# Two products instead of three in the channel-major gemms, full-height score and decay products, and a hand-written start, in a three-layer hybrid block

## The chip, the cores and the metric

One core of a Trainium2 chip runs the whole program; the other cores are idle. The metric is device time in microseconds (us) of one execution. A run of the kernel before was timed three times: 1604.77, 1605.06 and 1608.36 us, median 1605.06. A separate execution was profiled.

## The reference, cut to what matters

The model has 256 tokens of width 1024 and batch 1. Two layers each do `x + 0.5*swiglu(norm(x))`, a mixer, and a second half-weight swiglu; the hidden width is 2816. The first mixer is a gated linear recurrence with 4 heads, the second is attention in a window of 128 tokens with 16 query heads and 2 key heads of width 64; both also attend to 256 memory tokens. A third layer is a state-space scan with 32 heads in 4 groups, beside a short convolution, followed by one more swiglu. All of it is fp32. These lines are the ones that the change touches:

```python
# first mixer: scores with a running maximum of the gates
log_d = b[..., :, None] - b[..., None, :] + ic[..., None, :]
s = jnp.einsum('bhjd,bhsd->bhjs', qc, kc) * jnp.exp(log_d - m_t[..., None])
# second mixer, per block of 128 queries: 8 query heads share a key head
s = jnp.einsum('bqhgd,bkhd->bhgqk', qn, kn)
# third layer: causal convolutions, and decays within the scan
xbc = jax.nn.silu(causal_depthwise_conv(xbc, ssd_conv_w) + ssd_conv_b)
seg = acum[:, :, None] - acum[:, None, :]
decay = jnp.exp(jnp.where(causal, seg, -jnp.inf))
v = causal_depthwise_conv(s_c * s_x, sconv_w)
```

## The kernel before, in words

Every weight matrix is read once from HBM, in 520 or so chunks of up to 512 KB, by SP's queue into five `raw` buffers (`load`, lines 312 to 319). `prepare` (lines 321 to 330) splits a chunk: ACT rounds it to the fast format fp32r (`whi`), DVE subtracts to get the remainder (`wlo`); there are nine buffers of each. Activations are split the same way. A product of two split numbers is made of three products, hi by hi, hi by lo and lo by hi, added up in PSUM.

There are three kinds of gemm. `gemm` (line 392) is token-major: it loads 128x128 of the activations as the stationary operand and streams 512 columns of weights past it, three times (lines 423 to 425). `gemm_ch` (line 434) is channel-major: the weights are stationary, and 256 tokens are streamed. Its three products for one tile of 128 channels are lines 445 to 447, and it goes through the four chunks in order, k-tile by k-tile, with all four tiles of 128 channels open in two PSUM banks; the evacuation functions get these banks at the end of the call. It is called 14 times: for a_q and a_k of the first mixer (lines 915 and 916), and for B, C, xs0 to xs3 and two times three parts of `sconv` in the third layer. `gemm_hidden` (line 564), used by the gated feed-forward (`ffn_in`), is channel-major too, but goes tile by tile: for one tile it passes through all four chunks, with one product of 512 columns (weights' hi by the operand's hi and lo side by side, line 574) and one of 256 (weights' lo by the operand's hi, line 575). One bank then holds two halves, which `both_parts` adds: a copy on ACT (line 600) and an addition on DVE.

`bank(mm)` gives one of four PSUM banks for gemms, and four more serve all else (`sm`). 31 slots of 128x512 in SBUF serve activations.

Order of work: the program is written out as one list. Elementwise and small matrix work of the mixers stands in generators that `tick` and `pump` advance, so that it is interleaved with the gemms at a set pace (`pace`), and `defer` puts a step off by a number of ticks. The framework's scheduler then orders each engine's queue by these places and by when it expects operands to be ready; a later instruction with free operands can be put ahead. What is decided at build time stays: each engine works its queue in order.

Around the small products that the change touches: `score_head` (line 854) broadcasts a head's gate maxima with a product of four rows (line 857, fp32, which goes as two passes). `swa_units` (line 1039) makes scores by products of 64 rows, one per head (line 1061, fp32, two passes); even and odd heads lie on the lower and upper 64 partitions, and a unit takes heads of one parity; the keys lie twice in `bkt`, once for each half (line 1022). `ssd_unit` (line 1266) spreads the cumulated decays of two heads to all partitions with two products of 64 rows (line 1278): `act_t` holds a hi and a lo part of each of 32 heads, and `pick` selects and adds them.

The first instructions (lines 751 to 776): SP loads token block 0 of x, the gain row, the first chunks and block 1; TensorE does 8 warm-up products, the products that spread the gain row (line 766), and 12 more; `norm_residual` norms and splits both token blocks; `ffn_in` begins with a group of 8 chunks (`FIRST`), first for token block 0, then for block 1.

Of the kernel before, what the change touches and what calls it, by code (L numbers as in the profile page):

```python
# [10 lines left out]
F32 = mybir.dt.float32  # L11
# [6 lines left out]
P = 128  # L18
# [67 lines left out]
def hybrid_kernel(ctx: ExitStack, tc: tile.TileContext, *aps, names=None):  # L86
# [58 lines left out]
    act.copy(out=identr, in_=ident)  # L145
# [175 lines left out]
    def prepare(upto):  # L321
        while prepared[0] < min(upto, len(plan)):
            c = plan[prepared[0]]
            load(prepared[0] + RAW)
            prepared[0] += 1
            c.hi = wpool.tile([P, 1024], F32R, tag="whi", bufs=WBUFS, name=nm("whi"))
            c.lo = wpool.tile([P, 1024], F32R, tag="wlo", bufs=WBUFS, name=nm("wlo"))
            n = max(off + w for _, _, off, w in c.entries)
            act.copy(out=c.hi[:, 0:n], in_=c.raw[:, 0:n])  # L329
            tt(c.lo[:, 0:n], c.raw[:, 0:n], c.hi[:, 0:n].bitcast(F32), ALU.subtract)  # L330
# [102 lines left out]

    def gemm_ch(chunks, xop, evac):

        ps = [bank(mm), bank(mm)]
        nk = 8
        for c in chunks:
            need(c)
            for kt, key, off, n in c.entries:  # L440
                xh, xl = xop.mov(kt)
                for j in range(n // P):
                    o = ps[j // 2][:, (j % 2) * SEQ:(j % 2 + 1) * SEQ]
                    wh, wl = c.hi[:, off + j * P:off + (j + 1) * P], c.lo[:, off + j * P:off + (j + 1) * P]
                    pe.matmul(out=o, lhsT=wh, rhs=xh, start=kt == 0 and j % 2 == 0, stop=False)  # L445
                    pe.matmul(out=o, lhsT=wh, rhs=xl, start=False, stop=False)  # L446
                    pe.matmul(out=o, lhsT=wl, rhs=xh, start=False, stop=kt == nk - 1 and j % 2 == 1)  # L447
                tick()
            used[0] += 1
        for i in range(2):  # L450
            evac(i, ps[i])
# [112 lines left out]
    def gemm_hidden(chunks, xop, tiles, evac):  # L564


        for i in range(tiles):
            ps = bank(mm)
            for c in chunks:
                if i == 0:  # L570
                    need(c)
                for kt, _, off, _ in c.entries:
                    sl = slice(off + i * P, off + (i + 1) * P)
                    pe.matmul(out=ps, lhsT=c.hi[:, sl], rhs=xop.both(kt), start=kt == 0, stop=False)  # L574
                    pe.matmul(out=ps[:, 0:SEQ], lhsT=c.lo[:, sl], rhs=xop.mov(kt)[0], start=False, stop=kt == 7)  # L575
                if i == tiles - 1:
                    used[0] += 1
# [870 lines left out]
```

## Time and profile before

| | |
|---|---|
| runs | 1604.77, 1605.06, 1608.36 us; median 1605.06 |
| the profiled execution | 1604.94 us, span 1603.2 us |
| TensorE matmuls | 1583.9 us busy, 99% of the span, 8664 records |
| weight loads (PEld) | 1355.3 us, 85% |
| DVE, ACT, POOL | 65%, 55%, 2% of the span |
| HBM | 176 GB/s over the span |

The span goes from the first to the last instruction; the execution's own time also holds what lies outside it. PE is TensorE, PEld its weight loads, which run beside the products. Products are pipelined: each is recorded with its whole latency, so that neighbours overlap, and the cost of one in a dense stream is the distance to the next start. An fp32 product appears as two records. In a timeline equal neighbours are merged, with their number behind the x; a bracket tells how long the engine stood idle before the row and what ended it.

### The profile page before, as it was taken

To read this page: it belongs to the slowest core of one execution; us is meant where nothing else is said; L and a number is where in the kernel's file an instruction comes from. 1 tells how busy PE (TensorE), PEld (TensorE's weight loads), DVE (VectorE), ACT (ScalarE), POOL (GpSimd) and SP (SyncE) were. 2 spreads that over 40 slices of the span, in tenths; PEclk is the share of its full clock that TensorE was granted. 3 is DMA by queue.
4 is the path that set the end of the run, shared out by engine and by line. 5 is a ranking of instruction groups with operands and counts; after the bars stand their busy time and mean duration, and the time that the engine had idled before them with its cause. 6 is when DMAs were issued, how large, how long until landed. Compare 5 with 4: busy or idle time off the path is not lost.

```text
span 1603.2 us, 22953 instructions
## 1 busy us (share of the span) xinstructions
PE 1583.9 (99%) x8664; PEld 1355.3 (85%) x8664; DVE 1037.7 (65%) x1632; ACT 886.1 (55%) x1430; POOL 39.7 (2%) x72
## 2 busy tenths in 40 slices
PE   8999999999999999999999999999999999999998
PEld 7888897788888888887788888889899988888886
DVE  6676475657765567747765676468788864577662
ACT  6665365546655455635565655357855653456542
POOL 1000000100000000001100000000000000000000
PEclk9999999999999999999999999999999999999999
DMA  8656374446556546564323666465455566565560
GB/s 281 196 179 229 117 261 143 151 132 210 174 194 223 179 163 202 193 215 165 119 79 115 200 200 223 143 217 180 146 157 154 151 195 185 157 211 170 197 223 28
DMA packets 126467, 282.89 MB, mean 176 GB/s; under 512 B 11774, under 2 KB 23186, under 8 KB 126356
## 3 DMA queue, kind: packets, MB, share of 16 engines
q1 hardware_dynamic: 126356, 281.43, 54.6%
q8 instruction: 68, 1.11, 0.3%
q14 instruction: 43, 0.35, 0.1%
HBM read 280.34 MB, written 1.05 MB: 176 GB/s over the span
## 4 chain that ended last, share of the span: by engine, by line
PE 93%; DVE 2%; issue 1%; DMA 1%; ACT 1%; POOL 1%; SPq 0%; POOLq 0%; DVEq 0%; ACTq 0%
PE ps L574 20%; PE ps L423 15%; PE ps L425 15%; PE ps L424 15%; PE ps L575 11%; PE ps L445 3%; PE ps L446 3%; PE ps L447 3%; PE ps L458 2%; PE ps L1061 1%; PE ps L1303 1%; PE ps L676 1%; POOL t L517 1%; DVE wlo L122 1%; PE ps L1083 1%
## 5 line engine op out<-in xcount | busy, mean ns | idle before, releaser
L122 DVE TENSOR_TENSOR wlo<-raw,whi 128x1024 fp32r<-128x1024 f32 (+1 forms) x521 | 626.2, 1212 | 228.9 <-ACT whi L329 222.3
L329 ACT CAST whi<-raw 128x1024 fp32r<-128x1024 f32 (+1 forms) x521 | 537.5, 1042 | 321.8 <-PE ps L425 226.6
L574 PE MATMUL ps<-xt,whi 128*128 128x512 f32 x1440 | 500.6, 392 | 0.0
L575 PE MATMUL ps<-xt,wlo 128*128 128x256 f32 x1440 | 403.2, 280 | 0.0
L574 PEld LDWEIGHTS ps<-xt,whi 128*128 128x128 f32 x1440 | 269.4, 187 | 59.1
L423 PE MATMUL ps<-whi,s 128*128 128x512 f32 x696 | 277.4, 400 | 0.3 <-ACT s L1380 0.3
L424 PE MATMUL ps<-wlo,s 128*128 128x512 f32 x696 | 274.4, 394 | 0.0
L425 PE MATMUL ps<-whi,s 128*128 128x512 f32 x696 | 274.1, 394 | 0.0
L575 PEld LDWEIGHTS ps<-xt,wlo 128*128 128x128 f32 x1440 | 272.2, 189 | 0.2
L122 DVE TENSOR_TENSOR s<-ps,s 128x256 f32<-128x256 f32 (+1 forms) x218 | 101.3, 468 | 120.3 <-ACT s L600 100.8
L423 PE MATMUL ps<-whi,xt 128*128 128x512 f32 (+2 forms) x448 | 174.2, 389 | 3.2 <-ACT xt L460 1.8
L425 PE MATMUL ps<-whi,xt 128*128 128x512 f32 (+2 forms) x448 | 170.1, 381 | 1.2 <-DVE xt L122 1.2
L424 PE MATMUL ps<-wlo,xt 128*128 128x512 f32 (+2 forms) x448 | 169.8, 379 | 0.0
L423 PEld LDWEIGHTS ps<-whi,s 128*128 128x128 f32 x696 | 130.8, 188 | 31.4 <-DVE s L122 0.8
L425 PEld LDWEIGHTS ps<-whi,s 128*128 128x128 f32 x696 | 130.7, 188 | 30.7
L424 PEld LDWEIGHTS ps<-wlo,s 128*128 128x128 f32 x696 | 130.9, 188 | 28.7
L445 PE MATMUL ps<-xt,whi 128*128 128x256 f32 x448 | 129.1, 288 | 0.0
L122 DVE TENSOR_TENSOR s<-s,s 128x256 f32<-128x256 f32 (+2 forms) x228 | 107.7, 478 | 32.5 <-ACT s L616 18.0
L446 PE MATMUL ps<-xt,whi 128*128 128x256 f32 x448 | 127.0, 284 | 0.0
L447 PE MATMUL ps<-xt,wlo 128*128 128x256 f32 x448 | 126.8, 284 | 0.0
L600 ACT COPY s<-ps 128x256 f32<-128x256 f32 x180 | 66.2, 368 | 86.7 <-PE ps L575 84.8
L423 PEld LDWEIGHTS ps<-whi,xt 128*128 128x128 f32 x448 | 84.4, 188 | 19.9 <-ACT xt L460 2.2
(218 smaller groups left out, 1369.3 us busy)
## 6 DMA issues: line engine op xcount, KB each, us to landing
raw<-in_ffn_w_in_dram SPq DMA_DIRECT2D x160, 512.0 KB, 4.9
raw<-in_ffn_w_out_dram SPq DMA_DIRECT2D x88, 512.0 KB, 4.5
raw<-in_w_in_dram SPq DMA_DIRECT2D x80, 512.0 KB, 3.9
raw<-in_a_w_in_dram SPq DMA_DIRECT2D x24, 512.0 KB, 4.4
raw<-in_w_down_dram SPq DMA_DIRECT2D x22, 512.0 KB, 4.8
raw<-in_ffn_w_in_dram SPq DMA_DIRECT2D x32, 256.0 KB, 4.5
raw<-in_w_ssd_proj_dram SPq DMA_DIRECT2D x16, 512.0 KB, 3.6
raw<-in_w_gate_dram SPq DMA_DIRECT2D x16, 512.0 KB, 5.0
```

The source lines that it names most:

```text
L122: (eng or dve).tensor_tensor(out=o, in0=a, in1=b, op=op)
L329: act.copy(out=c.hi[:, 0:n], in_=c.raw[:, 0:n])
L423: pe.matmul(out=o, lhsT=xh, rhs=wh, start=first, stop=False)
L424: pe.matmul(out=o, lhsT=xh, rhs=wl, start=False, stop=False)
L425: pe.matmul(out=o, lhsT=xl, rhs=wh, start=False, stop=last)
L445: pe.matmul(out=o, lhsT=wh, rhs=xh, start=kt == 0 and j % 2 == 0, stop=False)
L446: pe.matmul(out=o, lhsT=wh, rhs=xl, start=False, stop=False)
L447: pe.matmul(out=o, lhsT=wl, rhs=xh, start=False, stop=kt == nk - 1 and j % 2 == 1)
L458: pe.transpose(out=ps[:, i * P:(i + 1) * P], in_=src[:, i * P:(i + 1) * P], identity=ident)
L574: pe.matmul(out=ps, lhsT=c.hi[:, sl], rhs=xop.both(kt), start=kt == 0, stop=False)
L575: pe.matmul(out=ps[:, 0:SEQ], lhsT=c.lo[:, sl], rhs=xop.mov(kt)[0], start=False, stop=kt == 7)
L600: act.copy(out=dst, in_=ps[:, SEQ:2 * SEQ])
```

## The change

`gemm_ch` becomes a wrapper around the tile-by-tile loop, now called `gemm_tiles`; each tile is evacuated by `parts_sum` into an SBUF slot, and the former evacuation functions read the slot. The products for decays, gate maxima and scores get 128 rows: with cleared rows in `m_t`, `acs`, `act_t`, `pick`, and with keys in cleared tiles `kpad`, where the keys of one head half stand in 64 rows of one column block and again in the other 64 rows of a second block, so that one product serves two heads. Scores now work with hi and lo parts (three fp32r products). `identr` is filled later. The first instructions of TensorE, ACT and DVE are kept in the order written; the gain row is loaded from ACT's queue; `x`'s second block is loaded ahead of chunks 2 to 4; the first `ffn_in` begins with a group of 3 chunks, then one chunk at a time.

```diff
     def prepare(upto):
         while prepared[0] < min(upto, len(plan)):
...
+            prepare_hi()()
+
+    def prepare_hi():
...
+        act.copy(out=c.hi[:, 0:n], in_=c.raw[:, 0:n])
+        return lambda: tt(c.lo[:, 0:n], c.raw[:, 0:n], c.hi[:, 0:n].bitcast(F32), ALU.subtract)
...
+    def parts_sum(dst, ps):
+
+        act.copy(out=dst, in_=ps[:, SEQ:2 * SEQ])
+        tt(dst, ps[:, 0:SEQ], dst, ALU.add)
+
+    def gemm_tiles(chunks, xop, tiles, evac):
+
+
+        for i in range(tiles):
+            ps = bank(mm)
+            for n_c, c in enumerate(chunks):
+                if i == 0:
+                    need(c)
+                for n_k, (kt, _, off, _) in enumerate(c.entries):
+                    sl = slice(off + i * P, off + (i + 1) * P)
+                    pe.matmul(out=ps, lhsT=c.hi[:, sl], rhs=xop.both(kt), start=kt == 0, stop=False)
+                    pe.matmul(out=ps[:, 0:SEQ], lhsT=c.lo[:, sl], rhs=xop.mov(kt)[0], start=False, stop=kt == 7)
+                if i == tiles - 1:
+                    used[0] += 1
+                if n_c == 1 or n_c == 3:
+                    tick()
+            evac(i, ps)
+
     def gemm_ch(chunks, xop, evac):
...
+        pair = []
+
+        def tile_evac(i, ps):
+            if i % 2 == 0:
+                pair.append(slot())
+            parts_sum(pair[-1][:, (i % 2) * SEQ:(i % 2 + 1) * SEQ], ps)
+            if i % 2 == 1:
+                evac(i // 2, pair[-1])
+        gemm_tiles(chunks, xop, 4, tile_evac)
...
-    def ffn_in(blocks, xop):
+    def ffn_in(blocks, xop, ahead=FIRST):
...
-        gemm(blocks[0], xop, evac, [blocks[0][0:FIRST], blocks[0][FIRST:]] if FIRST < 8 else [blocks[0]])
+        gemm(blocks[0], xop, evac, [blocks[0][0:ahead]] + [[c] for c in blocks[0][ahead:]])
...
-        nc.sync.dma_start(out=g_row[j * 32:j * 32 + 1, :], in_=A["ffn1_norm_g"][0:1, j * 512:(j + 1) * 512])
-    prepare(2)
+        nc.scalar.dma_start(out=g_row[j * 32:j * 32 + 1, :], in_=A["ffn1_norm_g"][0:1, j * 512:(j + 1) * 512])
+    load(2)
     load_x(1)
+    load(RAW)
...
+    with tc.manual_schedule(engines={mybir.EngineType.PE, mybir.EngineType.Activation, mybir.EngineType.DVE}):
+        warm_up(WARM[0])
...
+        warm_up(WARM[1])
+        halves = {}
+        normed(res_half(0), gains, halves.__setitem__)
+        for j in range(2):
+            low = prepare_hi()
+            split_t(halves[j], 4, [xop.hi[j][:, :, 0, :], xop.lo[j][:, :, 0, :]])
+            xop.filled.add((0, j))
+            low()
+        act.copy(out=identr, in_=ident)
+        norm_residual(1, gains, xop)
...
-    h = ffn_in(S["f1in0"], xop)
+    h = ffn_in(S["f1in0"], xop, 3)
...
-    def q_evac(i, ps):
-        s = slot()
-        act.activation(out=s, in_=ps, func=AF.Copy, scale=float(P) ** -0.5)
+    def q_evac(i, s):
+        act.activation(out=s, in_=s, func=AF.Copy, scale=float(P) ** -0.5)
...
-        pe.matmul(out=bc[:, 0:SEQ], lhsT=ident[0:4, hh:hh + 1].to_broadcast([4, P]), rhs=m_t[0:4, 0:SEQ],
+        pe.matmul(out=bc[:, 0:SEQ], lhsT=ident[:, hh:hh + 1].to_broadcast([P, P]), rhs=m_t[:, 0:SEQ],
...
+    kpad = [[slot(F32R).rearrange("p (u t) -> p u t", u=2) for _ in range(2)] for _ in range(2)]
+    for kp in kpad[0] + kpad[1]:
+        pool_e.memset(kp.bitcast(F32), 0.0)
...
+            for u in range(2):
+                rows_u = slice(64 * u, 64 * u + 64)
+                for g in range(2):
+                    kh, kl = (kp[rows_u, u, t * P:(t + 1) * P] for kp in kpad[g])
+                    kt = tk[rows_u, g * P:(g + 1) * P]
+                    act.copy(out=kh, in_=kt)
+                    tt(kl, kt, kh.bitcast(F32), ALU.subtract)
...
+                qh, ql = slot(F32R), slot(F32R)
+                act.copy(out=qh, in_=tq)
+                tt(ql, tq, qh.bitcast(F32), ALU.subtract)
...
-        sets = [[h0 + par + 2 * i for i in range(per)] for h0 in range(0, 8, 2 * per) for par in range(2)]
+        sets = [list(range(h0, h0 + per)) for h0 in range(0, 8, per)]
...
+            for i in range(0, per, 2):
+                pair = slice((hs[i] // 2) * P, (hs[i] // 2 + 1) * P)
+                o2 = s[:, i * w:(i + 2) * w].rearrange("p (a b) -> p a b", a=2)
+                pe.matmul(out=o2, lhsT=qh[:, pair], rhs=kh, start=True, stop=False)
+                pe.matmul(out=o2, lhsT=qh[:, pair], rhs=kl, start=False, stop=False)
+                pe.matmul(out=o2, lhsT=ql[:, pair], rhs=kh, start=False, stop=True)
...
-            pe.matmul(out=sb[:, i * SEQ:(i + 1) * SEQ], lhsT=pick[:, hd:hd + 1].to_broadcast([64, P]), rhs=act_t,
+            pe.matmul(out=sb[:, i * SEQ:(i + 1) * SEQ], lhsT=pick[:, hd:hd + 1].to_broadcast([P, P]), rhs=act_t,
...
-        def sc_evac(i, ps):
-            s = slot()
-            act.copy(out=s, in_=ps)
+        def sc_evac(i, s):
             pr.append(s)
```

## Rows read from the trace of the kernel before

**Rows 1.** The page: busy time of each engine, and the chain that ended last.

```profile
PE 1583.9 (99%) x8664; PEld 1355.3 (85%) x8664; DVE 1037.7 (65%) x1632; ACT 886.1 (55%) x1430; POOL 39.7 (2%) x72
PE 93%; DVE 2%; issue 1%; DMA 1%; ACT 1%; POOL 1%; SPq 0%; POOLq 0%; DVEq 0%; ACTq 0%
```

**Rows 2.** Windows: length, then PE, PEld, DVE, ACT, POOL busy; clock, DMA share, GB/s.

```profile
1180.00:1260.00 80.00, 79.96 (x631) 75.86 (x631) 70.63 (x125) 51.35 (x90) 4.96 (x5) 1.00 0.54 154
...
213.00:238.00 25.00, 22.68 (x187) 22.00 (x187) 20.90 (x48) 14.85 (x22) 1.57 (x2) 1.00 0.94 334
...
1272.00:1320.00 48.00, 47.73 (x220) 38.90 (x218) 29.23 (x35) 24.23 (x31) 1.48 (x2) 1.00 0.63 196
```

**Rows 3.** Timeline of the start: start us, us, engine, line, operation, out<-in, count.

```profile
5.57 0.55 POOL L513 TENSOR_TENSOR t<-t,mhalf 128x1 f32<-128x1 f32 x1 [2.31 <-DVE pick L122]
6.19 1.44 PE L766 MATMUL ps<-s,ones 1*128 1x512 f32 x4
8.65 0.74 DVE L131 SCALAR_TENSOR_TENSOR s<-xres,t,ps 128x512 f32<-128x512 f32 x1
9.67 0.60 PE L458 MATMUL ps<-ident,s 128*128 128x128 f32 x4
11.79 0.50 PE L423 MATMUL ps<-whi,xt 128*128 128x512 f32 x1 [1.51 <-ACT xt L460]
...
37.35 0.39 PE L574 MATMUL ps<-xt,whi 128*128 128x512 f32 x1
```

**Rows 4.** TensorE's timeline in the channel-major gemm, first and last of 22 groups.

```profile
223.15 0.28 PE L445 MATMUL ps<-xt,whi 128*128 128x256 f32 x1
...
231.07 0.28 PE L445 MATMUL ps<-xt,whi 128*128 128x256 f32 x1
```

**Rows 5.** TensorE's timeline in the gated feed-forward, first and last of 33 pairs.

```profile
42.37 0.39 PE L574 MATMUL ps<-xt,whi 128*128 128x512 f32 x1
...
53.81 0.39 PE L574 MATMUL ps<-xt,whi 128*128 128x512 f32 x1
```

**Rows 6.** TensorE's timeline around decay products.

```profile
1178.61 0.28 PE L445 MATMUL ps<-xt,whi 128*128 128x256 f32 x1
1178.82 0.50 PE L1278 MATMUL ps<-act_t,pick 64*128 64x256 f32 x2
1179.25 0.39 PE L446 MATMUL ps<-xt,whi 128*128 128x256 f32 x1
...
1125.74 0.73 PE L1278 MATMUL ps<-act_t,pick 64*128 64x256 f32 x4
1126.41 0.50 PE L423 MATMUL ps<-whi,xt 128*128 128x512 f32 x1
```

**Rows 7.** TensorE's timeline around scores.

```profile
771.53 1.16 PE L1061 MATMUL ps<-s,s 64*128 64x128 f32 x8 [0.67 <-DVE s L1022]
772.61 0.50 PE L425 MATMUL ps<-whi,xt 128*128 128x512 f32 x1
...
778.10 0.70 PE L1061 MATMUL ps<-s,s 64*128 64x256 f32 x2
778.73 0.44 PE L676 MATMUL ps<-ident,s 128*128 128x128 f32 x2
```

**Rows 8.** TensorE's timeline around gate maxima; then the chain (start, us, what).

```profile
246.09 0.69 PE L857 MATMUL ps<-s,ident 4*128 4x256 f32 x2
246.72 0.50 PE L424 MATMUL ps<-wlo,xt 128*128 128x512 f32 x1
...
308.52 1.79 PE ps L719 x8
```

**Rows 9.** Groups by line and form: busy us, mean ns, idle time before.

```profile
L122 DVE TENSOR_TENSOR s<-ps,s 128x256 f32<-128x256 f32 x180 | 75.9, 422 | 101.0 <-ACT s L600 100.8
L600 ACT COPY s<-ps 128x256 f32<-128x256 f32 x180 | 66.2, 368 | 86.7 <-PE ps L575 84.8
```

**Rows 10.** TensorE's timeline in the channel-major gemm of a_q, at a wait.

```profile
222.06 0.33 PE L676 MATMUL ps<-ident,s 128*128 128x128 f32 x1 [1.76 <-DVE s L122]
```

More of the change, by code (lines that the diff above doesn't have):

```diff
@@ L144, in hybrid_kernel @@
     identr = const.tile([P, P], F32R, name="identr")
-    act.copy(out=identr, in_=ident)
     ones = const.tile([P, P], F32, name="ones")
@@ L322, in prepare @@
         while prepared[0] < min(upto, len(plan)):
[L323 to L330, printed above, removed]
+            prepare_hi()()
+    def prepare_hi():
+        c = plan[prepared[0]]
+        load(prepared[0] + RAW)
+        prepared[0] += 1
+        c.hi = wpool.tile([P, 1024], F32R, tag="whi", bufs=WBUFS, name=nm("whi"))
+        c.lo = wpool.tile([P, 1024], F32R, tag="wlo", bufs=WBUFS, name=nm("wlo"))
+        n = max(off + w for _, _, off, w in c.entries)
+        act.copy(out=c.hi[:, 0:n], in_=c.raw[:, 0:n])
+        return lambda: tt(c.lo[:, 0:n], c.raw[:, 0:n], c.hi[:, 0:n].bitcast(F32), ALU.subtract)
     index = {}
@@ L562, in norm_after @@
         return dst, lambda t: norm_residual(t, gains, dst)
[L564 to L577, printed above, removed]
-                if c is chunks[1] or c is chunks[3]:
-                    tick()
-            evac(i, ps)
-    def ffn_in(blocks, xop):
+    def ffn_in(blocks, xop, ahead=FIRST):
         h = Operand()
@@ L798, in hybrid_kernel @@
     m_t = slot()
+    pool_e.memset(m_t[:, 0:SEQ], 0.0)
     def gate_chain():
@@ L1057, in unit @@
             o = slot()
-            cols = slice(hs[0], hs[-1] + 1, 2)
-            for i, hh in enumerate(hs):
-                half = slice(64 * (hh % 2), 64 * (hh % 2) + 64)
-                pe.matmul(out=s[:, i * w:(i + 1) * w], lhsT=qt[half, (hh // 2) * P:(hh // 2 + 1) * P],
-                          rhs=bkt[half, g * SEQ:g * SEQ + w], start=True, stop=True)
+            cols = slice(hs[0], hs[-1] + 1)
+            kh, kl = (kp[:, :, 0:w] for kp in kpad[g])
+            for i in range(0, per, 2):
[4 more added lines that the diff above has]
+                pe.matmul(out=o2, lhsT=ql[:, pair], rhs=kh, start=False, stop=True)
             for i, hh in enumerate(hs):
@@ L1321, in sconv @@
         pr, vv = [], []
-        def sc_evac(i, ps):
-            s = slot()
-            act.copy(out=s, in_=ps)
+        def sc_evac(i, s):
             pr.append(s)
```

67 lines of the change are left out of this document (20 added, 47 removed).

## The prediction

> **What bounds the kernel now.** I began with the page's table of engines and its chain of waits [rows 1]. TensorE's matmul row is busy for 1583.9 us of a span of 1603.2 us, and 93% of the chain that ends last is TensorE; DVE has 2% and DMA 1%. So the kernel is a stream of matrix products with few holes, and a change counts as far as it shortens that stream or opens a hole in it. How long a record lasts says little, since the records overlap; I read prices as the distance from one start to the next in TensorE's timeline. The windows by stage came next, to see where DVE, which works beside TensorE, has room [rows 2]: the granted clock is 1.00 there, the upper level of 2.4 GHz, and DVE is busy for 70.6 of 80 us in the state-space stretch. Last I read the first microseconds [rows 3].
>
> The profiled execution took 1604.94 us, beside a median of 1605.06; the sum below is made from 1604.94, and what lies outside the span (1.7 us) stays.
>
> **Three products become two.** gemm_ch is called 14 times (a_q, a_k, B, C, four xs, six of sconv), each with 8 k-tiles by 4 tiles: 448 groups of three 256-column products. From the L445 at 223.15 to the one at 231.07 lie 22 groups, 7.92 us: 0.360 us a group [rows 4]. The new loop issues what the gated feed-forward already does, one 512-column and one 256-column product: from 42.37 to 53.81 lie 33 pairs, 11.44 us: 0.347 us a pair [rows 5]. The columns are the same 768; one weight load and one instruction go. 448 times 0.0133 us is **6.0 us**, all of it on TensorE's stream. The Trainium skill, TensorE: Matmul & The Clock Gate, "Back-to-back issue gap", gives columns / 2.4 plus 2.5 ns for a product at the upper clock; by that a group would cost 327.5 ns and a pair 324.9, so the term would be 1.2 us. Both rows are dearer than that, and the row decides.
>
> **Decays on 128 rows.** ssd_unit issues two 64-row products of 256 columns, in 16 units. Around one of them, L445 at 1178.61, the pair at 1178.82 and L446 at 1179.25 [rows 6]: 0.64 us, of which a lone L445 would take 0.12. The pair costs 0.52. Two of 128 rows and 256 columns cost 0.24 by [rows 4]. Where four stand in a row the price is lower: 0.67 us from 1125.74 to 1126.41, 0.34 a pair. So the gain is 0.10 to 0.28 a unit, 1.6 to 4.5 us; most units stand alone, with an entry and an exit each, and I take **4.4**.
>
> **Scores.** For t = 0 a unit scores four heads: eight passes, 1.08 us from 771.53 to 772.61; for t = 1 one head takes two passes, 0.63 us from 778.10 to 778.73 [rows 7]. To each run comes an entry of 0.09, as L445 shows ahead of the decays (0.21 where it takes 0.12). There are 4 units of the first kind, 4.7 us, and 16 heads of the second, 16 times 0.63 or 10.1 us plus some entries. After, two heads share three products: 256 columns wide at t = 0, 8 pairs by 3 by 0.12 = 2.9 us, and 512 wide at t = 1, 8 by 3 by 0.23 (a pair [rows 5] less 0.12) = 5.5 us. The gain is 14.8 less 8.4, **6.4 us** without the entries of the second kind; 4 to 7.5 as bounds, according to how many entries go.
>
> **Gate maxima.** Four heads have a four-row product of two passes: 0.63 us each plus 0.09 [rows 8]. Eight passes of the 128-row fp32 product of the same width take 1.79 us, 0.22 each [rows 8]. Four times (0.72 less 0.45) is **1.0 us**; 0 to 1.2.
>
> **First instructions.** Now the scale of the norm is known at 6.12 (POOL, 5.57 plus 0.55), but the first normalised half is only started at 8.65, since DVE splits weights first; transposes run at 9.67, the first real product at 11.79 and the first L574 at 37.35 [rows 3]. Hand-ordered, the gain row comes on ACT's queue, the eight warm-up products lead to the gains' product (now 6.19) a little earlier, twelve more follow, and the transposes can start near 8.6: 3.5 us behind the gains, as now, and 1 us sooner. Then some 0.45 for them and 0.6 for the copy: first product near 10, 1.8 us earlier. Against it, DVE now makes the operand's lo ahead of the weights' lo (1.2 us), and chunk 1 is behind in turn, so TensorE will wait once or twice before 16 us. On SP's queue two loads of x move ahead of chunks 2 to 4, each of which lands about 1 us later; the gain row's two issues go from SP to ACT, ahead of squares that wait for x anyway. Groups of 3 chunks ask for token block 1 after 18 products (4.1 us), where now 48 precede it, but need each later chunk half as fast. I take **1.5 us**; bounds -1 and 4.
>
> **What is added.** 56 tiles get a copy on ACT and an addition on DVE: 0.37 and 0.42 us each [rows 9], 21 and 24 us, less six plain evacuations that go. In the state-space stretch 1180 to 1260 DVE is busy for 70.6 us [rows 2]; 21 tiles add 8.9, 79.5 in all, while TensorE's time there shrinks to about 75.5. DVE is then 4 us over. What can give way is the scan's own elementwise work: its results are needed by ssd_proj alone, after sconv_proj and gb, and there DVE is busy for 29.2 of 48 us [rows 2]. Weight splits are made a call ahead. I charge **2.0 us**; bounds 0 and 8. For a_q and a_k DVE goes from 20.9 of 25 us [rows 2] to 24.3, where TensorE already waits 1.76 us for DVE in front of a transpose [rows 10]: charge **1.0**, bounds 0 and 3.4. In the windowed attention four hi/lo splits of q (at most 0.84 each on DVE, twice the addition [rows 9]) and eight small ones of k are added, the latter in the chain that TensorE waits 0.67 us for at 771.53 [rows 7]: charge **0.7**, bounds 0 and 2. Cleared tiles and the wider m_t cost POOL alone, which is busy for 2% [rows 1]. The ticks that pace side work stay 8 a call.
>
> **Sum.** 6.0 + 4.4 + 6.4 + 1.0 + 1.5 = 19.3 off, 3.7 on: 15.6. 1604.94 less 15.6 is 1589.3; I say **1589 us**.
>
> **The rivals.** *DVE costs its bounds* (0.16): the three charges reach 8, 3.4 and 1 us and the first instructions bring nothing. 17.8 off, 12.4 on: 1599.5. For it speaks the stretch at 88% of DVE before anything is added; against it, that TensorE has no hole there now.
>
> *More than forecast* (0.12): no charge is due, since a tile's evacuation no longer comes in a lump behind the call, and the start brings 4: 21.8 off, 1583.
>
> *The page's spacing* (0.05): the group costs no more than columns, the 0.0133 us were interference; 1.2 in place of 6.0 gives 1594. Against it stand 22 and 33 repeats [rows 4, 5].
>
> *The padding does not do it* (0.06): what 64 rows cost extra comes from the fp32 scores or the broadcast column and not from the rows. Decays and maxima (5.4) stay: 1594.7. Against it, both entry and exit are dear only around the narrow products [rows 6]. The Trainium skill, TensorEngine Tiling (Array Packing), "Key Properties", speaks against the change in another way: tiles of 64 rows can run beside one another, which padding gives up. Eight passes in 1.08 us, 0.135 each, show no two at once; had they run so, the scores would come out 1 us dearer and the time near 1597.
>
> *Slower* (0.04): the four banks for products. A tile now keeps its bank until DVE has added its two parts. Three tiles, 8.3 us, is the slack; if the scan's work sits ahead of the sum for longer than that, TensorE stops at the fifth tile. At 2.5 us for each of the ten calls of the scan it is 25 us on, 1589 + 25 = 1614 us. The feed-forward runs the same evacuation with no such stop, but DVE has 65% of the span as a whole [rows 1].
>
> Several small mishaps at once (0.04) would leave no change.
>
> **How the numbers follow.** The forecast has 0.52 and spans 1585 to 1593. A measurement here can tell 0.3%, 4.8 us. Of the first rival a quarter (0.04) lies above 1600.2, with the mishaps 0.08 for the same; slower is 0.04; faster is the rest, 0.88. The range 1581 to 1600 takes in the forecast with its bounds, the larger gain and most of the first rival, and leaves out about 0.15.
>
> **What would show it.** Right: L447 gone and 448 pairs 0.347 apart; decay products 0.12 apart with no entry; scores with three products a pair of heads; the first product near 10 and the first paired product near 36; DVE near 100% from 1170 to 1250 with TensorE's idle time under 3 us there. Wrong: holes in TensorE in front of weight splits or transposes in that stretch, pairs at 0.36, or a start where TensorE waits on DVE past 17 us.

## The result: 0.6% slower, and the profile after

The changed kernel takes 1615.3 us (median of four runs, 1614.22 to 1616.23) beside 1605.15 for the kernel before: a ratio of 1.0056, 95% interval 1.0041 to 1.0071. Forecast were 1589 us and a gain; the time lies outside the range. The profiled execution took 1616.23 us, 11.3 more than that of before.

The page of the changed kernel, engines and chain, answers to [rows 1]:

```profile
PE 1583.1 (98%) x8200; PEld 1332.7 (83%) x8200; DVE 1058.5 (66%) x1698; ACT 904.8 (56%) x1492; POOL 44.4 (3%) x78
...
PE 88%; DVE 5%; ACT 3%; issue 2%; DMA 1%; POOL 1%; POOLq 0%; ACTq 0%; DVEq 0%; SPq 0%
```

464 records are gone, but TensorE's share of the chain has fallen from 93 to 88%, and DVE and ACT have gone from 2 and 1 to 5 and 3. So the stream now has holes. Its windows, to be read beside [rows 2], show where:

```profile
1180.00:1260.00 80.00, 73.32 (x432) 62.62 (x431) 69.97 (x132) 51.78 (x98) 3.65 (x5) 0.98 0.44 137
216.00:250.00 34.00, 29.43 (x163) 24.93 (x162) 24.15 (x59) 19.36 (x35) 2.66 (x12) 0.95 0.70 234
1200.00:1220.00 20.00, 15.38 (x83) 12.92 (x83) 19.32 (x37) 12.76 (x31) 1.10 (x2) 0.91 0.56 164
1280.00:1330.00 50.00, 49.66 (x221) 40.38 (x220) 34.10 (x46) 25.49 (x35) 2.94 (x2) 0.97 0.61 192
```

From 1180 to 1260 TensorE stands for 6.7 us, where it had 0.04 before. In the worst 20 us DVE is busy for 19.32, and TensorE for 15.38 at a granted clock of 0.91. TensorE's timeline there:

```profile
1209.72 0.28 PE L453 MATMUL ps<-xt,wlo 128*128 128x256 f32 x1
1211.35 0.50 PE L1293 MATMUL ps<-act_t,pick 128*128 128x256 f32 x2 [1.35 <-DVE s L122]
1215.11 0.80 PE L452 MATMUL ps<-xt,whi 128*128 128x512 f32 x1 [3.27 <-DVE s L122]
...
1215.92 0.63 PE L452 MATMUL ps<-xt,whi 128*128 128x512 f32 x1
...
1216.56 0.63 PE L452 MATMUL ps<-xt,whi 128*128 128x512 f32 x1
...
1218.46 0.39 PE L452 MATMUL ps<-xt,whi 128*128 128x512 f32 x1
1218.69 0.28 PE L453 MATMUL ps<-xt,wlo 128*128 128x256 f32 x1
1218.81 0.40 PE L452 MATMUL ps<-xt,whi 128*128 128x512 f32 x1
```

And DVE's at the same time:

```profile
1210.54 0.15 DVE L126 TENSOR_SCALAR t<-t 128x1 f32<-128x1 f32 x1 [0.48 <-ACT junk L1277]
1210.61 0.68 DVE L122 TENSOR_TENSOR s<-ps,s 128x512 fp32r<-128x512 f32 x1
1211.36 0.75 DVE L131 SCALAR_TENSOR_TENSOR s<-s,t,s 128x512 f32<-128x512 f32 x1
1212.03 1.22 DVE L122 TENSOR_TENSOR wlo<-raw,whi 128x1024 fp32r<-128x1024 f32 x1
1213.16 0.15 DVE L126 TENSOR_SCALAR t<-t 128x1 f32<-128x1 f32 x1
1213.23 0.68 DVE L122 TENSOR_TENSOR s<-ps,s 128x512 fp32r<-128x512 f32 x1
1213.97 0.75 DVE L131 SCALAR_TENSOR_TENSOR s<-s,t,s 128x512 f32<-128x512 f32 x1
1214.64 0.75 DVE L122 TENSOR_TENSOR s<-ps,s 128x256 f32<-128x256 f32 x2
```

The sums of two tiles (last row) stand in DVE's queue behind the scan's finishing steps, which wait in turn for ACT (L1277); the next tile gets its bank at 1215.11. The 3.4 us behind the two waits run at the lower clock, 1.2 GHz: pairs start 0.64 apart (1215.92 to 1216.56) in place of 0.35. That costs 1.7 us more, and it happens three times in this execution (from 225.2, 1215.0 and 1279.9), each time after a hole; in the kernel before it happens nowhere between the start and the end.

The table gives the stages of the profiled executions, each from its first product with the weights' remainder (wlo) to the first of the next stage. "again" is a second profiled execution of the changed kernel; no_add, tiles_three and tiles_three_start ("..._start") are experiments described below. The short product of the scan's steps (dt) is counted with B.

| stage, us | before | after | again | no_add | tiles_three | ..._start |
|---|---|---|---|---|---|---|
| first feed-forward pair at | 37.6 | 38.0 | 35.5 | 35.5 | 38.1 | 37.6 |
| a_q, a_k | 28.5 | 32.7 | 30.9 | 30.3 | 28.7 | 28.8 |
| a_v | 30.9 | 28.1 | 28.1 | 28.4 | 28.4 | 28.0 |
| attention | 64.1 | 61.4 | 61.7 | 61.4 | 61.3 | 61.3 |
| B, C, xs0, xs1 | 51.0 | 50.3 | 50.2 | 49.9 | 50.7 | 50.7 |
| z1 | 29.0 | 29.3 | 29.4 | 27.7 | 28.8 | 28.8 |
| scan (xs2 to sb1) | 120.1 | 125.3 | 125.8 | 114.9 | 115.4 | 115.4 |
| sconv_proj | 25.7 | 27.5 | 25.9 | 25.8 | 25.8 | 25.8 |
| feed-forward 1 | 100.6 | 102.5 | 102.5 | 102.5 | 102.5 | 100.6 |
| feed-forward 2 | 100.4 | 100.4 | 100.4 | 100.4 | 100.4 | 100.4 |
| feed-forward 3 | 100.4 | 102.2 | 102.2 | 102.2 | 100.4 | 100.4 |
| feed-forward 4 | 100.4 | 100.4 | 100.4 | 102.2 | 100.4 | 100.4 |
| feed-forward 5 | 100.4 | 102.2 | 102.2 | 100.4 | 100.4 | 100.4 |

Part of what the two executions of the changed kernel differ by is where the lower clock falls: the second has no such stretch in a_q, a_k and sconv_proj (30.9 and 25.9 us in place of 32.7 and 27.5), and in the scan one of 6.8 us, from 1209.9, in place of 3.4.

### The profile page after: what moved, and what is told of

The parts are those of the page before. It is cut to its first block, busy times and chain, and to the rows that moved or that the text cites. A ratio compares the mean times of both kernels' runs of the same rounds, so it can differ in the third digit from the quotient of the medians.

```text
span 1614.5 us, 22147 instructions
## 1 busy us (share of the span) xinstructions
PE 1583.1 (98%) x8200; PEld 1332.7 (83%) x8200; DVE 1058.5 (66%) x1698; ACT 904.8 (56%) x1492; POOL 44.4 (3%) x78
## 4 chain that ended last, share of the span: by engine, by line
PE 88%; DVE 5%; ACT 3%; issue 2%; DMA 1%; POOL 1%; POOLq 0%; ACTq 0%; DVEq 0%; SPq 0%
PE ps L452 25%; PE ps L426 15%; PE ps L428 15%; PE ps L427 15%; PE ps L453 13%; DVE wlo L122 2%; PE ps L477 2%; DVE s L122 1%; ACT whi L332 1%; POOL t L536 1%; DVE s L131 1%; PE ps L673 1%; DMA raw<-in_w_in_dram 1%; PE ps L760 1%; PE ps L1318 1%
## 5 line engine op out<-in xcount | busy, mean ns | idle before, releaser
L332 ACT CAST whi<-raw 128x1024 fp32r<-128x1024 f32 (+1 forms) x521 | 536.5, 1042 | 285.2 <-PE ps L428 221.4
L452 PE MATMUL ps<-xt,whi 128*128 128x512 f32 x1888 | 669.9, 399 | 4.6 <-DVE s L122 3.9
L452 PEld LDWEIGHTS ps<-xt,whi 128*128 128x128 f32 x1888 | 355.8, 188 | 89.3 <-DVE s L122 3.5
L453 PEld LDWEIGHTS ps<-xt,wlo 128*128 128x128 f32 x1888 | 357.9, 190 | 1.0 <-issue 0.7
L122 DVE TENSOR_TENSOR s<-ps,s 128x256 f32<-128x256 f32 (+2 forms) x286 | 128.9, 456 | 128.3 <-ACT s L439 107.3
L439 ACT COPY s<-ps 128x256 f32<-128x256 f32 x236 | 85.5, 370 | 96.2 <-PE ps L453 95.3
L122 DVE TENSOR_TENSOR s<-s,s 128x256 f32<-128x256 f32 (+2 forms) x236 | 113.2, 486 | 36.6 <-ACT s L613 18.9
L426 PEld LDWEIGHTS ps<-whi,xt 128*128 128x128 f32 x448 | 84.2, 188 | 18.2 <-DVE s L122 1.4
L427 PEld LDWEIGHTS ps<-wlo,xt 128*128 128x128 f32 x448 | 84.3, 188 | 16.7 <-DVE wlo L122 2.1
L428 PEld LDWEIGHTS ps<-whi,xt 128*128 128x128 f32 x448 | 84.2, 188 | 16.1 <-DVE xt L122 0.2
L613 ACT CAST s<-s 128x256 fp32r<-128x256 f32 x90 | 36.4, 404 | 56.5 <-DVE s L122 56.5
```

What stands on the lines that cost most here:

```text
L122: (eng or dve).tensor_tensor(out=o, in0=a, in1=b, op=op)
L426: pe.matmul(out=o, lhsT=xh, rhs=wh, start=first, stop=False)
L427: pe.matmul(out=o, lhsT=xh, rhs=wl, start=False, stop=False)
L428: pe.matmul(out=o, lhsT=xl, rhs=wh, start=False, stop=last)
L439: act.copy(out=dst, in_=ps[:, SEQ:2 * SEQ])
L613: act.copy(out=a, in_=u)
```

## The experiments

Ratios are to runs of the kernel before beside them (medians 1605.4 to 1607.1). Where the spacing of the feed-forwards differs, the stage decides and not the time.

**One part at a time.** old_ch is the changed kernel with the former gemm_ch and its evacuations, only_ch the kernel before with the new gemm_ch alone, in which each call becomes:

```diff
+            parts_sum(pair[-1][:, (i % 2) * SEQ:(i % 2 + 1) * SEQ], ps)
+        gemm_tiles(chunks, xop, 4, tile_evac)
```

> The changed kernel (1615.3 us) with the former three-product gemm_ch and its evacuation; scores, decays, maxima and the new start stay. Theory 1, the additions on DVE: in the scan and in a_q/a_k DVE gets 24 us of work back, TensorE's waits of 1 us and more there go, and with them the half-rate stretches at 1215 and 1280; 8 to 10 us less in 1120 to 1310, the total near 1602. Theory 2, the wide scores and the start made the loss: the scan stays about as late, total 1612 or more. Theory 3, the full-height products made it: as theory 2 in the scan.

> The kernel before (1605.15) with the new gemm_ch alone. Theory 1: the loss shows here by itself, waits in the scan and in a_q/a_k eat more than the 6 us of the two products; total 1608 to 1614. Theories 2 and 3: the 6 us are kept, total near 1599 to 1602.

old_ch: 1602.27 us, 0.9978 (0.9968 to 0.9989), scan 116.2. only_ch: 1620.59, 1.0085 (1.007 to 1.01), scan 129.1, a_q and a_k 33.5, dearer still than the 1608 to 1614 expected. The two-product form is the whole loss; the rest of the change gains.

narrow_wide has only the decays and maxima, old_ch_start also the scores, both with the old start and the old gemm_ch:

```diff
-    act_t = const.tile([64, SEQ], F32R, name="act_t")
+    act_t = const.tile([P, SEQ], F32R, name="act_t")
```

> The kernel before with the 128-row decays and gate maxima alone. The prediction's terms, 4.4 and 1.0: 5.4 us off the kernel before, and nothing but the scan (120.1 us before, about 116 here) and the first mixer's gate units shorter; bounds 1.6 and 5.7. If the feed-forward blocks come out 1.8 us longer or shorter than in the kernel before (100.4 or 102.3 us each), that is their spacing and not this edit, and the stage lengths decide, not the time.

> Decays and maxima as in narrow_wide, and the scores of pairs of heads; three products and the start of before. The prediction's term for scores: 6.4 us less than narrow_wide, less 0.7 charged. What the trace of the changed kernel makes me expect: attention 64.1 to 61.4 us, so 2.7 us only, since new waits for ACT and DVE in front of the value products give back about half. Against old_ch, which has the new start, it should be 1.5 to 2 us slower if the new start is worth what its own trace shows there (first paired product at 35.9 in place of 37.6).

narrow_wide: 1602.0, 0.9966 (0.9954 to 0.9979), that is 5.5 us; the scan goes from 120.1 to 116.2, a_q to a_v from 59.4 to 57.6. Here, as in old_ch_start, one later feed-forward block is 1.8 us longer than before (below). old_ch_start: 1598.84, 0.995 (0.9935 to 0.9965), attention 61.3: the scores are worth 2.7 us. It beats old_ch, which has the new start, though part of that is the spacing of the feed-forwards (two later long blocks in old_ch, one here). By stages old_ch reaches its first pair 1.8 us sooner (35.9 against 37.7) and has a first block that is 1.9 us longer, so the new start gains nothing on balance.

**Which part of the two-product form?** no_add leaves out the addition of the two halves; tiles_three goes by tiles, but with three products of 256 columns into one half bank.

```diff
-            parts_sum(pair[-1][:, (i % 2) * SEQ:(i % 2 + 1) * SEQ], ps)
+            act.copy(out=pair[-1][:, (i % 2) * SEQ:(i % 2 + 1) * SEQ], in_=ps[:, 0:SEQ])
```

```diff
+                    pe.matmul(out=o, lhsT=c.hi[:, sl], rhs=xh, start=kt == 0 and i % 2 == 0, stop=False)
+                    pe.matmul(out=o, lhsT=c.hi[:, sl], rhs=xl, start=False, stop=False)
+                    pe.matmul(out=o, lhsT=c.lo[:, sl], rhs=xh, start=False, stop=kt == 7 and i % 2 == 1)
```

> The changed kernel with the DVE addition of gemm_ch left out: the second half of each bank, weights' hi by the operand's lo, is not added, a copy on ACT stays; TensorE's products are all there. Theory 1: DVE loses 24 us, waits in the scan fall below 3 us in total, total near 1604. Theory 2b, the order by tiles is to blame (four chunks wanted within the first tile), not the addition: the waits stay, total 1612 or more.

> The changed kernel with gemm_ch tile by tile, but three 256-column products into one half bank and the former evacuation, so no sum of parts. Theory 1: no waits to speak of, only the 6 us of the second product are lost: total near 1602 to 1606. Theory 2b, the order by tiles: waits in front of weight splits stay, total 1612 or more.

no_add: 1600.57, 0.9962 (0.9947 to 0.9977). tiles_three: 1596.78, 0.994 (0.9925 to 0.9955), both better than expected. Without the addition 10.4 of the scan's 125.3 us go, without the second half of the bank 9.9. The order by tiles is no cause; it even gains (against old_ch 0.8 us in the scan and 1.0 from a_q to a_v, and loses 0.4 in z1). In no_add a pair still costs more than forecast: where the scan's stream runs on, its wide products are 232 ns apart on average and its narrow ones 117, so 349 and not 347. With those that come behind other products it is 236 and 118, so 354.

**Load, bank or latency?** Three kernels take something off DVE, or the bank off it.

```diff
-SEG_ACT = 2
+SEG_ACT = 4
```

> The changed kernel with four in place of two of the scan's exponent inputs made on ACT, some 11 us of DVE's work in the scan moved; the two products and their sums on DVE stay. Theory (late sums on DVE stop TensorE, and the clock falls after the stop): the scan falls from 125.3 us to 116 to 119, the half-clock stretches at 1215 and 1280 are gone, a_q and a_k stay at 32.7 with theirs, and the time is 6 to 9 us under the changed kernel, 1606 to 1609. Rival (the form of the two products or their bank order costs it, whoever is busy): the scan stays at 124 to 126 and the time at 1615. Second rival (ACT becomes the late one, since it also copies each tile): the holes stay and end on ACT.

```diff
-            parts_sum(pair[-1][:, (i % 2) * SEQ:(i % 2 + 1) * SEQ], ps)
+            tmp = slot()
+            act.copy(out=tmp, in_=ps)
+            tt(pair[-1][:, (i % 2) * SEQ:(i % 2 + 1) * SEQ], tmp[:, 0:SEQ], tmp[:, SEQ:2 * SEQ], ALU.add)
```

> The changed kernel, but in gemm_ch ACT copies a tile's whole bank to SBUF and DVE adds the two halves there: DVE does the same 56 additions in the same places, yet a bank comes free without it. Theory A (the addition stands in DVE's queue behind the scan's finishing steps, which wait for ACT and POOL in turn, and the bank waits for it): the holes before first products of a tile go; the scan falls from 125.5 to 115 to 118 us, a_q and a_k from 31 to 32.7 to about 30, the time to 1600 to 1605. Theory B (DVE has simply too much to do in these stretches): the holes stay, in front of transposes or decays if not of tiles, the scan stays above 122, and the time at 1611 or more. seg_act4, where DVE had less and the scan stayed at 125.7, speaks against B.

(pool_sum has the same copy, and `pool_e.tensor_tensor` in place of `tt`.)

> As bank_act, but POOL, which is busy for 2% of the span, adds the halves from SBUF, so DVE has no sums of gemm_ch at all. Theory A: as bank_act or a little shorter, scan 115 to 117, 1598 to 1603, since the products of transposes no longer wait for a sum behind others on DVE. Theory B: the gain comes only here and not in bank_act. Against both: an addition on POOL may last several times 0.42 us or hold up DVE beside it, and then a_q and a_k, whose results are awaited, stay at 31 or more.

The hopes for less time missed in all three: seg_act4 1612.86 (1.0037, 1.0024 to 1.005), scan 125.7; bank_act 1614.28 (1.006, 1.0044 to 1.0076), scan 125.7; pool_sum 1617.7 (1.0068, 1.0049 to 1.0086), scan 123.2 and z1 3.2 longer. seg_act4 was a weak test: windows over the scan, of the changed kernel run again and of seg_act4, show that DVE lost 2.5 us and not 11, while ACT gained 8:

```profile
1150.90:1276.70 125.80, 117.40 (x688) 100.62 (x687) 107.47 (x199) 86.09 (x159) 4.21 (x6) 0.97 0.47 148
```

```profile
1151.40:1277.10 125.70, 118.46 (x693) 101.64 (x692) 105.02 (x179) 94.33 (x182) 4.77 (x6) 0.97 0.49 151
```

In bank_act the wait for the bank moved to ACT. Its TensorE rows, then those of ACT:

```profile
1211.29 0.48 PE L1295 MATMUL ps<-act_t,pick 128*128 128x256 f32 x2
...
1213.99 0.50 PE L452 MATMUL ps<-xt,whi 128*128 128x512 f32 x1 [2.11 <-ACT s L468]
```

```profile
1209.90 2.94 ACT L332 CAST whi<-raw 128x1024 fp32r<-128x1024 f32 x3
1212.75 0.63 ACT L1279 ACTIVATE junk<-s 128x512 f32<-128x512 f32 x1
1213.28 0.19 ACT L1279 ACTIVATION_READ_ACCUMULATOR junk<-s 128x1 f32 x1
1213.37 0.57 ACT L468 COPY s<-ps 128x512 f32<-128x512 f32 x1
```

The copy stands in ACT's queue behind three casts of weights and the squares of the scan's norm, one after the other without a pause. So the bank waits for whichever queue is to free it; that its release by DVE alone is the loss (theory A) is refuted, and the numbers are those of theory B. pool_sum misses both theories: its banks wait for ACT's copy as well, and though DVE has no sums there, it is busy for 104.2 us of the scan, 7.0 more than in no_add, since its own steps became dearer. By groups of DVE in the scan, no_add and pool_sum:

```profile
L131 DVE SCALAR_TENSOR_TENSOR s<-s,pcol,s 128x254 f32<-128x254 f32 x16 | 7.3, 477 | 0.1
L128 DVE TENSOR_SCALAR s<-ps,t 128x128 f32<-128x128 f32 x20 | 5.9, 343 | 0.0
```

```profile
L131 DVE SCALAR_TENSOR_TENSOR s<-s,pcol,s 128x254 f32<-128x254 f32 x16 | 8.8, 573 | 0.1
L128 DVE TENSOR_SCALAR s<-ps,t 128x128 f32<-128x128 f32 x20 | 5.9, 338 | 0.0
```

Of the steps on SBUF alone some take up to a fifth longer on average beside the additions on POOL (0.99 us each), while the plain products of two 128x512 operands (686 and 681 ns) and the steps with a PSUM operand do not. The Trainium skill, SBUF — State Buffer, "Who interferes with whom", names a port pair shared by DVE and GpSimd as the only place of contention; that the steps with a PSUM operand stay agrees with it.

The last pair is to tell load from latency. lean_dve takes other work off DVE (it leaves out the remainders of some weights) and keeps the sums; three_dummy is tiles_three with as many useless additions:

```diff
+        if id(c) in lean:
+            c.lo = c.hi
+            return lambda: None
```

> The changed kernel, in which the first of four chunks of each channel-major call is not split: its remainder is left out and the hi part stands in for it, so DVE has 14 subtractions of about 1.2 us less (2 beside a_q and a_k, 8 in the long channel-major stretch of the scan, 9.7 us there), while all sums, copies, banks and products stay. seg_act4 moved 21 instructions, but only 2.5 us of DVE's time (105.0 in place of 107.5 us in that stretch), so it tested DVE's load weakly. Theory B (load: DVE's work does not fit in time beside TensorE's shorter stream): the scan falls from 125.8 to 115 to 118 us, a_q and a_k from 31 to 33 to about 29, time 1599 to 1604. Theory C (latency: each tile's result is later by a copy and an addition, and what consumes it stands at fixed places in TensorE's queue): the scan stays above 122, time above 1609.

```diff
                 evac(i // 2, ps)
+                for u in range(2):
+                    tt(slot()[:, 0:SEQ], ps[:, u * SEQ:(u + 1) * SEQ], mask_a, ALU.add)
```

> tiles_three with 56 useless additions on DVE, two per finished pair of tiles behind its evacuation, each of a bank's half and a constant into a slot that nobody reads: the load of the sums without the sums being awaited. Theory B (load): the scan rises from 115.4 to 121 to 126 us, a_q and a_k from 28.7 to 30 to 33, time 1605 to 1612. Theory C (latency of the awaited result): the scan stays at 115 to 117, time 1597 to 1600.

three_dummy: 1615.44, 1.0056 (1.0042 to 1.007), as slow as the changed kernel, with three products and a result that nobody awaits. Its scan takes 123.6 us, z1 35.8 and sconv_proj 26.9, together 16.3 more than in tiles_three; a_q and a_k stay at 28.6. lean_dve: 1604.81, 0.9986 (0.9976 to 0.9996), dearer than theory B said. Counted like the others, its scan takes 120.2, and its window is

```profile
1150.20:1270.40 120.20, 115.51 (x692) 99.06 (x691) 101.00 (x193) 84.99 (x157) 4.78 (x6) 1.00 0.49 153
```

With 6.5 us less work on DVE than in the second execution of the changed kernel, and all sums kept, the scan is 5.5 us shorter: TensorE idles for 4.7 in place of 8.4 us, and no stretch runs at the lower clock. So DVE's load does at least half of it; in what is left DVE still has 101.0 us of work, where no_add has 97.3. three_dummy speaks for load too, but less purely: its additions read the bank, so the bank, if not their result, is awaited. TensorE stops for over 4 us here, until a bank's useless additions (1249.64, 0.75 us) are done. TensorE, then DVE:

```profile
1245.87 0.28 PE L474 MATMUL ps<-xt,wlo 128*128 128x256 f32 x1
1250.44 0.58 PE L472 MATMUL ps<-xt,whi 128*128 128x256 f32 x1 [4.29 <-DVE s L122]
```

```profile
1244.99 1.23 DVE L122 TENSOR_TENSOR wlo<-raw,whi 128x1024 fp32r<-128x1024 f32 x1 [0.75 <-ACT whi L332]
1247.17 1.00 DVE L131 SCALAR_TENSOR_TENSOR s<-ps,pcol,s 128x255 f32<-128x255 f32 x2 [0.96 <-ACT s L1217]
1248.11 1.23 DVE L122 TENSOR_TENSOR wlo<-raw,whi 128x1024 fp32r<-128x1024 f32 x1
...
1249.64 0.75 DVE L122 TENSOR_TENSOR s<-ps,mask_a 128x256 f32<-128x256 f32 x2
```

DVE even idles here for 0.75 and 0.96 us, waiting for ACT: at this load the two queues, each in order, wait for one another. In none of the profiles is DVE busy for more than 87% of the scan. Where TensorE has no holes it is 84 to 87% (before, tiles_three, old_ch). Where TensorE waits, more work on DVE makes a longer scan and no higher share, 84 to 86%: 101.0 us of 120.2 in lean_dve, 103.5 of 123.6 in three_dummy, 105.0 of 125.7 in seg_act4, 107.7 of 125.3 in the changed kernel.

In a_q and a_k the clock blurs the stage lengths. The windows over this stage, of no_add and of the second execution of the changed kernel (the third number from the right is the granted clock):

```profile
213.60:243.90 30.30, 27.81 (x158) 23.80 (x157) 20.23 (x49) 17.73 (x32) 2.67 (x12) 0.94 0.74 253
```

```profile
213.60:244.50 30.90, 26.64 (x157) 22.63 (x157) 22.77 (x56) 18.00 (x33) 2.66 (x12) 1.00 0.73 247
```

no_add has 3.4 us at the lower clock there (from 222.6), and so has lean_dve (from 231.1), worth some 1.7 us each. TensorE's idle time tells more: 4.6 and 4.3 us in the two executions of the changed kernel, 2.5 in no_add, 2.6 in lean_dve, 1.8 in tiles_three and three_dummy, 2.3 before. So leaving out the additions, or two weight splits, takes most of the added waits away here too, while three_dummy's additions, which stand behind the evacuation, add none. That what counts here is DVE's work ahead of an awaited result fits this, but no run isolates it.

**The feed-forward blocks.** Their code is unchanged, yet three of five are 1.8 to 1.9 us longer. The changed kernel was run again:

> The changed kernel unchanged, to see what varies between executions of one program. Theory: each feed-forward block is 100.4 or 102.3 us long, and which blocks are long differs from the profile of the changed kernel (there the first, third and fifth of the five), while the scan (125.3) and a_q with a_k (32.7) repeat within 0.5 us with their half-clock stretches. Rival: the long blocks belong to the program (where its instructions or buffers lie) and the same three are long again. Time 1614 to 1617.

1613.62, 1.004 (1.0027 to 1.0053). The rival holds: the same three blocks are long, so it belongs to the program. The scan repeats (125.8), but a_q and a_k do not (30.9), nor do the half-clock stretches, of which there is one in place of three. To the first pair the two executions differ by 2.5 us (38.0 and 35.5). Two products of the changed kernel with 35 pairs between them, in the second block:

```profile
404.95 0.39 PE L452 MATMUL ps<-xt,whi 128*128 128x512 f32 x1
...
417.08 0.40 PE L452 MATMUL ps<-xt,whi 128*128 128x512 f32 x1
```

and two with 35 in the third:

```profile
599.70 0.40 PE L452 MATMUL ps<-xt,whi 128*128 128x512 f32 x1
...
612.06 0.40 PE L452 MATMUL ps<-xt,whi 128*128 128x512 f32 x1
```

12.13 and 12.36 us, 347 and 353 ns a pair. In the one the wide product takes 230 to 233 ns, in the other 232, 240 and 236 in turn, over and over. ffn_cut breaks the stream:

```diff
+            if cut and i == 0:
+                pe.matmul(out=bank()[:, 0:P], lhsT=identr, rhs=identr, start=True, stop=True)
```

> The changed kernel with one product of 128 columns, whose result nobody reads, after the first tile of each of the nine calls in every feed-forward block: nine breaks of about 0.1 us a block. The blocks of 102.2 to 102.5 us consist of pairs whose wide products are 232, 241 and 236 ns apart in turn, those of 100.4 of pairs at 230 to 232 ns. Theory (an interruption of the stream lets the spacing change over, and the even one is kept until the next): the long blocks become 101 to 101.5 and the short ones 101.3, so the three-step spacing lasts for a tile or a few and not for a block. Rival (the spacing belongs to where the program's instructions lie, whatever comes between): the same three blocks stay long, 103.2, and the two others come to 101.3.

1618.69, 1.0077 (1.0058 to 1.0096). All blocks now take 102.2 to 102.9 us: the two spacings change over at the cuts, and a block has stretches of both. Half of each and nine cuts of 0.1 us make 101.4 + 0.9 = 102.3. So an interruption can switch the spacing, and it is then kept until the next, as the theory said, but into either one: in this run the even and the uneven one alternate from cut to cut, in all five blocks. Not every interruption switches it. Two transposes of parameters in the first block leave it even in the kernel before (at 54.5) and make it uneven in the changed kernel (at 60.9), where it stays so to the end of the block. What decides is open.

**The best version** is tiles_three with the start of before:

> Three products tile by tile, with decays, maxima and scores of the changed kernel, and the start of before. The traces show the new start reach the first paired product 1.8 us sooner, and the first feed-forward block 1.9 us longer behind it (102.5 in place of 100.6) in all six kernels with the new start. If the new start is worth nothing on balance, this kernel ties with tiles_three at 0.994 of before, within 0.001; by the term of the prediction (1.5) it would be 1.5 us slower, and if the spacing in the later blocks follows the start too, it could be 2 to 4 us faster (0.992).

> tiles_three_start unchanged, in more rounds: 0.9937 of before, within 0.0015; feed-forward blocks of 100.6 and four times 100.4 us again.

1594.52, 0.9937 (0.9921 to 0.9954), and again 1595.35, 0.9936 (0.9922 to 0.9949): the tie with tiles_three (0.994), 10.3 us less than before, and some 19 less than the changed kernel (1.0056 less 0.9936). All its later blocks are at 100.4 and the first at 100.6. It keeps decays, maxima, scores and the order by tiles, and drops the two-product form and the new start.

## Why the prediction was wrong, step by step

Stage by stage, forecast and found (after less before, us):

| part | forecast | found | difference |
|---|---|---|---|
| scan and sconv_proj | -3.4 - 4.4 + 2.0 = -5.8 | +7.0 | 12.8 |
| start, feed-forward 1 | -1.5 | +0.4 + 1.9 = +2.3 | 3.8 |
| feed-forwards 3 and 5 | 0 | +3.6 | 3.6 |
| attention | -6.4 + 0.7 = -5.7 | -2.7 | 3.0 |
| a_q, a_k, a_v | -0.9 - 1.0 + 1.0 = -0.9 | +1.4 | 2.3 |
| B, C, xs0, xs1, z1 | -1.7 | -0.4 | 1.3 |
| sum | -15.6 | +11.2 | 26.8 |

This is the profiled execution of the result. In the second one the sum is +6.2: start and first block make -0.2, a_q to a_v -0.4, attention -2.4, and scan with sconv_proj +5.8; the rest is as here.

**What is added: the step that failed.** I had the load right, DVE 4 us over in 80, and charged 2.0, with the sentence "What can give way is the scan's own elementwise work: its results are needed by ssd_proj alone". They are not: the scan's own transposes, decay and value products stand in TensorE's queue between the tiles, and wait for DVE at fixed places, and the gemm's banks wait behind the same queue. So DVE's delay became TensorE's at once. The sums cost 10.4 to 10.9 us in the scan (125.3 and 125.8 against 114.9 without them), outside my bound of 8. With them DVE needs 107.5 us (the window over the scan of the changed kernel run again) where TensorE needs 115, 93%; that average looks as if it fitted, but DVE, ACT and POOL wait for one another, this time is not in it, and no profile has DVE busy for more than 87% of the scan. The fall of the clock behind a hole was in no term: 1.7 us of the loss in the scan in the first execution, and again 1.7 in a_q with a_k and in sconv_proj, which the second execution was spared. For a_q and a_k I had charged 1.0: TensorE's idle time there grew by 1.9 to 2.3 us.

**Three products become two.** The mechanism holds, the size is half: against the three products of tiles_three, no_add is worth 0.5 us in the scan, and 1.1 more were lost to one hole (1229.1), in place of 3.4. That is 6 of the forecast 13 ns a pair. Where the stream runs on, a pair takes 349 and a group 359 ns, so the spacing explains 3 of the 7 ns that are missing; the others stay open. I read the pair from 33 repeats in the even spacing [rows 5], and did not see that the same kernel's first microseconds of that block were in the other. (One sum of the prediction is off by rounding: the 324.9 ns should be 325.0, and the term by it 1.1 us, not 1.2.)

**Decays, maxima: right.** 5.5 us by the time for a forecast of 5.4. That this is so near is in part luck, since one feed-forward block of narrow_wide is 1.8 us longer: by stages they gained 6.6, 3.9 in the scan and 0.9 from B to z1 for 4.4, and 1.8 in the first mixer for 1.0, a little over my bounds. Here only the rows changed, so the padding did it.

**Scores.** The products gained nearly what was forecast. Worked out as the distance to the next start beyond what is usual for the form, the holes of before in this stage (4.2 us) are still there with 3.4, and four new ones add 3.5: 2.7 net are 5.4 gross, for 6.4. The rival that the padding does not do it had no gain here, and falls with its price; but as the scores changed rows, format and pairing at once, no run shows which of these gained. Nor do the eight passes at 771.53 show that two halves of the array cannot run at once, as I read them: a unit's heads have one parity, so all eight lie on the same half. I had charged 0.7, for the first half's chain of k. The new waits come in the second half, before transposes and the first product behind the values, for ACT and DVE; four rows with the idle time of the changed kernel:

```profile
791.53 0.33 PE L673 MATMUL ps<-ident,s 128*128 128x128 f32 x1 [1.21 <-ACT s L1084]
...
797.65 0.44 PE L673 MATMUL ps<-ident,s 128*128 128x128 f32 x2 [0.20 <-ACT s L1084]
...
801.45 0.66 PE L673 MATMUL ps<-ident,s 128*128 128x128 f32 x4 [0.29 <-DVE s L122]
...
806.66 0.51 PE L426 MATMUL ps<-whi,s 128*128 128x512 f32 x1 [1.12 <-ACT s L479]
```

1.21 + 0.20 + 0.29 + 1.12 is 2.8 us of idle time, more with the latency of the product behind each. A shorter product brought the next wait forward: what was late next I had not looked for behind the gain.

**First instructions.** What I forecast came about, but not in the execution that the result was profiled in. The start of the changed kernel, to be read beside [rows 3], and then that of its second execution:

```profile
4.91 2.08 PE L765 MATMUL ps<-s,ones 1*128 1x512 f32 x4
6.92 4.45 PE L760 MATMUL ps<-ones 128*128 128x128 f32 x24
11.21 1.04 PE L477 MATMUL ps<-ident,s 128*128 128x128 f32 x8
12.48 0.73 PE L426 MATMUL ps<-whi,xt 128*128 128x512 f32 x2 [0.24 <-ACT xt L479]
14.34 0.50 PE L427 MATMUL ps<-wlo,xt 128*128 128x512 f32 x1 [1.12 <-DVE wlo L122]
```

```profile
4.91 1.13 PE L765 MATMUL ps<-s,ones 1*128 1x512 f32 x4
5.97 2.94 PE L760 MATMUL ps<-ones 128*128 128x128 f32 x24
...
10.03 0.73 PE L426 MATMUL ps<-whi,xt 128*128 128x512 f32 x2 [0.24 <-ACT xt L479]
```

The gains' products start early in both, as forecast. In the second execution the first product comes at 10.03, as forecast, and the first pair at 35.5. In the first the gains' products and the second warm-up take longer (2.08 and 4.45 us for 1.13 and 2.94), and all that follows is 2.5 us later. Which of the two an execution gets is chance as far as the runs show: of eleven profiles with the new start five have the first product at 9.7 to 10.4 and six at 12.4 to 13.9; of six with the old one five have it at 11.5 to 11.9 and one at 13.9. It looks like the lower clock, but the windows of both executions give a granted clock of 1.00 from 5 to 10 us, so this is not shown. On average over the profiles the first pair comes 1.5 us sooner with the new start (37.2 against 38.7). From the first product to the first pair next to nothing is saved (25.5 us, 25.8 before), as the forecast wait for a weight split costs 1.1 (14.34). Then the first block is 1.9 us longer in all nine kernels with the new start and no cuts (102.5), and in none with the old one (100.6 in six profiles), since it goes over to the uneven spacing on its way (at 60.9 in the changed kernel). That took the gain back.

**The rivals.** "Slower" had the number, 1614, and the place: TensorE stops at a tile whose bank DVE has not freed. As a mechanism it is half: bank_act shows that freeing the bank by ACT leaves the loss where it was, and in the changed kernel 3.9 of the scan's 8.5 us of idle time (3.27 at 1215.1 and 0.60 at 1249.0) are in front of a tile, the rest in front of the scan's own products and the first of sconv_proj. "DVE costs its bounds" was the same thought with too small a price.

## What to carry to other kernels

Before work is put on a helper engine in a stretch where it is busy for 85 to 90%, ask which of its results the bound engine awaits within that stretch; if any stand in between, the helper's queue is on the path, and work added to it can cost about its own duration: here DVE got 10.2 us more in the scan (107.5 against 97.3 in no_add), and the scan became 10.4 to 10.9 us longer. Price a saving of some nanoseconds an instruction from several stretches, not from one long clean one. And take a change of many parts apart: here decays, maxima and scores gained 8 us by the time, the start nothing on balance, and the last part gave back more than twice that.

## What was not expected of the hardware

After single holes in a stream that was otherwise dense (2.99 us at 224.5; 1.35 and 3.27 at 1211 and 1215), TensorE went on at half its clock for 3.4 us (granted clock 0.91 over 1200 to 1220), and such a hole cost 1.7 us more than it lasted. It is not each hole that does so: in no_add 0.98 and 0.82 us of idle time at 220.0 and 221.4 were followed by such a stretch, and 2.44 us at 221.6 in the second execution of the changed kernel were not. An unchanged stream of two products a pair runs at 347 or at 353 ns a pair, and keeps to one until something interrupts it: 1.8 us a block of 288 pairs, more than some parts of this change were worth. Additions on POOL made some of DVE's steps on SBUF a fifth longer on average (477 to 573 ns).
